# Splitting attention outputs at the accumulator, and one ring for raw weights and key tiles

## The chip, the cores and the metric

The kernel runs on one core of one Trainium2 chip. The metric is device time in microseconds. Of the kernel before there are three runs, and the median counts; one further execution was taken with a profile.

## The reference

Two layers (DEPTH = 2) over x of 2048 rows by 1024 columns, all in float32. Cut to what matters:

```python
for l in range(DEPTH):
    mod = silu(c) @ w_ada[l] + b_ada[l]
    shift, scale, gate = split(mod, 3)
    h = rms_norm(x, norm_g[l]) * (1 + scale) + shift
    gq, gk, gv, glr, gz, dq, dk, dv, dz = split_columns(h @ w_in[l])
    # group A: gated linear attention, 4 heads, chunks of 64 rows
    gq, gk, gv = split(silu(causal_depthwise_conv([gq, gk, gv], conv_w[l])))
    o_gla = gla_branch(gq, gk, gv, glr, gz, ...)     # scan over chunks, rms_norm, * silu(gz)
    # group B: differential softmax attention, 4 heads, two maps of 64 columns each
    q, k = rms_norm(dq) * 64 ** -0.5, rms_norm(dk)
    s = q @ k.T, masked to chunks up to the query's
    o = (softmax(s[map 0]) - lam * softmax(s[map 1])) @ dv
    o_diff = rms_norm(o) * (1 - lam_init) * silu(dz)
    x = x + gate * ([o_gla, o_diff] @ w_out[l])
```

## The kernel before

The 2048 rows are worked through in four blocks of 512 rows (u = 0 to 3) for each of two layers, eight blocks in all. Large products are made in three passes. Each float32 operand is split into a high part, rounded to fp32r, and a low part, the rest; TensorE adds high x high, high x low and low x high in one accumulator. The normalised input is kept so in hhi and hlo, the weights in a tile w, whose two halves are hi and lo.

**Weights.** In the first block of a layer (u = 0) `weights()` loads a raw tile of 128 by 512 from HBM, ScalarE (ACT) casts it into hi, GpSimd (POOL) subtracts to get lo, and the pair is stored to a buffer in HBM, called wd. The later blocks load the finished pair from wd. There are 72 such tiles in a layer: 8 for each of four attention heads (items 0 to 3), 8 for each of two groups of the gated branch (4 and 5), 8 for its gate (6), and 16 for the two halves of the output projection (7 and 8). Raw tiles have a ring of three (p_raw), finished ones a ring of four (p_w). One tile is one step of a projection: 12 matmuls of 128x512.

**A head of attention.** `head_evac` copies queries and keys out of the accumulators into rw, squares and sums them, takes the power -1/2 on POOL, and writes the normalised values into a new tile qk. `qk_gen` transposes these on TensorE, first the queries (g = 0), then the keys (g = 1), and splits them into qh and ql, and into a key tile Kt. `attn_gen` computes scores, softmax on DVE and ACT, and the product with the values. In later blocks it also loads the key tiles Kj of the earlier blocks. Kt and Kj share a ring of five (tag "K" of p_kv). At the end `to_oT` transposes the output of the head into an accumulator of the ring tp and ACT scales it into a tile oT.

**Output projection.** `out_gen` runs for block u after the input of the next block is prepared. It goes twice over eight oT tiles, once for each half of the output columns, and each time splits the tile again: ACT casts it into oh, DVE subtracts to get ol.

**Order.** The program is recorded by six streams (`run_streams`), which take turns by a clock of TensorE costs (`pe(0.65)` for a quarter of a step) and by events with a lag. For instance the transposes of a head wait in `qk_gen` for

```python
yield need("hev", key, hd, lag=6.0)
```

The recorded operations are then put in order for each engine by `Program.order`, a list scheduler with a cost model. Among the operations that are ready it takes the one recorded first. A tile of a ring gets a place only in the order in which the tiles were recorded, and only when an operation on it is ready otherwise:

```python
if b not in slot and (place[b] != nxt[t] or not slots[t]):
    blocked[t].append(i)
    break
```

Every engine, and the one DMA queue that SP issues, then works through its list strictly in that order. Most operations are recorded by `Program.issue`, so the profile gives nearly all of them line 284, and groups are told apart by the names of their tiles.

Of the kernel before, what the change touches and what calls it, by code (L numbers as in the profile page):

```python
# [11 lines left out]
F32 = mybir.dt.float32  # L12
F32R = mybir.dt.float32r
BF16 = mybir.dt.bfloat16
AF = mybir.ActivationFunctionType
ALU = mybir.AluOpType
# [4 lines left out]
P = 128  # L21
D = 1024
KT = D // P
UT = 512
# [4 lines left out]
C_GQ, C_GV, C_GLR, C_GZ, C_D = 0, 512, 1024, 1040, 1552  # L29
# [258 lines left out]
def trunk_kernel(ctx, tc, x, c, w_ada, b_ada, norm_g, w_in, conv_w, w_gk, b_gk, gla_norm_g,  # L288
# [10 lines left out]
    p_h = pool("p_h", 1)  # L299
    p_x = pool("p_x", 1)  # L300
    p_t = pool("p_t", 3)
    p_raw = pool("p_raw", 3)
    p_w = pool("p_w", 4)
    p_oT = pool("p_oT", 8)
    p_s = pool("p_s", 4)
    p_at = pool("p_at", 3)
    p_kv = pool("p_kv", 5)
    p_q = pool("p_q", 5)
# [209 lines left out]
    def run_streams(streams):  # L518
        st = [dict(g=g, ready=0.0, need=None) for g in streams]
        while st:  # L520
# [19 lines left out]
            else:  # L540
# [8 lines left out]
                assert nxt, [e["need"] for e in st]  # L549
                clock[0] = max(min(nxt), clock[0]) + 1e-6  # L550

    def weights(l, u, item, k, src, n=None):
        w = p_w.tile([P, 2, 512], F32R, tag="w", name="w")
        hi, lo = w[:, 0, :], w[:, 1, :]
        kept = WD[l][item][k]
        if u > 0:
            SY.dma_start(w.bitcast(F32), kept)
            return hi, lo
        raw = p_raw.tile([P, 512], F32, tag="raw", name="raw")
        SY.dma_start(raw if n is None else raw.rearrange("p (g n) -> p g n", n=n), src)  # L560
        A.copy(hi, raw)
        G.tensor_tensor(lo, raw, hi.bitcast(F32), op=ALU.subtract)
        if NU > 1:
            SY.dma_start(kept, w.bitcast(F32))
        return hi, lo
# [69 lines left out]
    def proj_T(l, u, item, col, banks):  # L635
        hhi, hlo = state["hhi"], state["hlo"]
        for k in range(KT):
            hi, lo = weights(l, u, item, k, w_in[l, k * P:(k + 1) * P, col:col + 512])
            for j in range(4):
                cs = slice(j * P, (j + 1) * P)  # L640
                if k == 0:
                    banks.append(acc())
                T.matmul(banks[j], hi[:, cs], hhi[k], start=(k == 0), stop=False)
                T.matmul(banks[j], hi[:, cs], hlo[k], start=False, stop=False)
                T.matmul(banks[j], lo[:, cs], hhi[k], start=False, stop=(k == KT - 1))
                yield pe(0.65)
# [17 lines left out]
    def to_oT(blocks, gain):  # L664
        ps = tp()
        for t in range(TT):
            T.transpose(ps[:, t * P:(t + 1) * P], blocks[t], ident)
        o2 = p_oT.tile([P, UT], F32, tag="oT", name="oT")
        A.activation(o2, ps, AF.Copy, scale=gain)
        return o2  # L670

    GL = {}

# [159 lines left out]
    oTs = {}  # L833
    HD = {}

    def head_evac(l, u, hd, banks):
        key = l * NU + u
        ss = p_sm.tile([P, TT, 4], F32, tag="qss", name="qss", bufs=2)
        rq = p_sm.tile([P, TT, 4], F32, tag="rq", name="rq", bufs=2)
        sz = p_z.tile([P, TT, P], F32, tag="z", name="z")  # L840
        Vt = p_kv.tile([P, TT, P], F32, tag="V", name="Vt")
        qk = []
        for t in range(TT):
            rw = p_t.tile([P, 256], F32, tag="rw", name="rw", bufs=4)
            A.copy(rw, banks[t][:, 0:256])
            th = p_t.tile([P, P], F32, tag="th", name="th", bufs=2)
            A.activation(th, banks[t][:, 384:512], AF.Tanh, scale=0.5)
            V.scalar_tensor_tensor(sz[:, t, :], th, 1.0, banks[t][:, 384:512], op0=ALU.add, op1=ALU.mult)
            A.copy(Vt[:, t, :], banks[t][:, 256:384])
            sq = p_t.tile([P, 256], F32, tag="sq", name="sq", bufs=2)  # L850
            A.activation(sq, rw, AF.Square)
            V.tensor_reduce(ss[:, t, :], sq.rearrange("p (a n) -> p a n", a=4), axis=AX.X, op=ALU.add)
            V.tensor_scalar(ss[:, t, :], ss[:, t, :], 1.0 / 64, EPS, op0=ALU.mult, op1=ALU.add)
            G.tensor_tensor(rq[:, t, :], ss[:, t, :], mhalf[:, 0:4], op=ALU.pow)
            n = p_q.tile([P, 256], F32, tag="qk", name="qk", bufs=4)
            V.tensor_tensor(n.rearrange("p (a n) -> p a n", a=4), rw.rearrange("p (a n) -> p a n", a=4),
                            rq[:, t, :].unsqueeze(2).to_broadcast([P, 4, 64]), op=ALU.mult)
            qk.append(n)
        HD[key, hd] = (qk, Vt, sz)

    def qk_gen(l, u, hd):
# [151 lines left out]
    def dense_gen(l, u, items):  # L1013
        key = l * NU + u
        yield need("h", key, lag=2.0)
        def gla_proj(grp):
            banks = []
            yield from proj_T(l, u, 4 + grp, C_GQ + 512 * grp, banks)
            if grp == 0:
                yield need("gate", key)  # L1020
            else:
                yield need("ktr", key)
            GL[f"cv{grp}"] = conv_evac(l, u, grp, banks)
            done("conv", key, grp)

        def head_proj(hd):
            def ld(k):
                src = w_in[l, k * P:(k + 1) * P, C_D:C_D + 2048].rearrange("p (g n) -> p g n", n=512)
                return weights(l, u, hd, k, src[:, :, hd * P:hd * P + P], n=P)

            banks = []
            yield from proj_N(ld, banks)
            if hd == LAST:
                done("free_h", key + 1)
            if hd >= 1:
                yield need("qkT", key, hd - 1)
            if hd >= 2:
                yield need("attn", key, hd - 2)
            head_evac(l, u, hd, banks)
            done("hev", key, hd)  # L1040

        def gate_proj():
            banks = []
            yield from proj_N(lambda k: weights(l, u, 6, k, w_in[l, k * P:(k + 1) * P, C_GZ:C_GZ + 512]), banks)
            if LAST == 4:
                done("free_h", key + 1)
            yield need("scan", key)
            osb = GL["osb"]
            for t in range(TT):
                sz = t2()  # L1050
                silu2(sz, banks[t])
                G.tensor_tensor(osb[:, t, :], osb[:, t, :], sz, op=ALU.mult)
            done("gz", key)

        LAST = 4
        for it in items:
            if it < 4:
                yield from head_proj(it)
            elif it < 6:
                yield from gla_proj(it - 4)  # L1060
            else:
                yield from gate_proj()

    def out_gen(l, u):
        y = layers[l]
        key = l * NU + u
        xsrc, xdst = io(l)
        final = key == L * NU - 1
        for hf in range(2):
            cs = slice(hf * 512, hf * 512 + 512)  # L1070
            banks = []
            for n_, k in enumerate((4, 5, 6, 0, 1, 2, 3, 7)):
                yield need("oT", key, 0 if k < 4 else k, lag=0.8)
                if n_ == 4:
                    rt = p_o.tile([P, TT, 512], F32, tag="osb", name="rt")
                    SY.dma_start(rt, xsrc(u)[:, cs].rearrange("(t p) n -> p t n", p=P))
                hi, lo = weights(l, u, 7 + hf, k, w_out[l, k * P:(k + 1) * P, cs])
                oh = p_oT.tile([P, UT], F32R, tag="oh", name="oh", bufs=2)
                ol = p_oT.tile([P, UT], F32R, tag="ol", name="ol", bufs=2)
                A.copy(oh, oTs[key, k])  # L1080
                V.tensor_tensor(ol, oTs[key, k], oh.bitcast(F32), op=ALU.subtract)
                for t in range(TT):
                    ts_ = slice(t * P, (t + 1) * P)
                    if n_ == 0:
                        banks.append(acc())
                    mm3(banks[t], oh[:, ts_], ol[:, ts_], hi, lo, n_ == 0, n_ == KT - 1)
                    yield pe(0.65)
            yield need("ada", l, 2)
            xo = xdst(u)[:, cs].rearrange("(t p) n -> p t n", p=P)
            for t in range(TT):  # L1090
                gy = t2()
                V.tensor_tensor(gy, banks[t], y.gate[:, cs], op=ALU.mult)
                if final and hf == 1:
                    V.tensor_tensor(rt[:, t, :], gy, rt[:, t, :], op=ALU.add)
                    SY.dma_start(xo[:, t, :], rt[:, t, :])
                    continue
                G.tensor_tensor(rt[:, t, :], gy, rt[:, t, :], op=ALU.add)
                if t % 2:
                    SY.dma_start(xo[:, t - 1:t + 1, :], rt[:, t - 1:t + 1, :])
        done("x", key)  # L1100
# [88 lines left out]
```

## Time and profile before

| | |
|---|---|
| median of 3 runs | 2660.28 us (2659.81 to 2660.94) |
| profiled execution | 2664.22 us |
| its span, first to last instruction | 2662.5 us |
| mean granted TensorE clock in it | 0.993 |
| TensorE (PE) busy | 2573.6 us, 97% |
| VectorE (DVE) busy | 1768.3 us, 66% |
| ScalarE (ACT) busy | 1207.0 us, 45% |
| GpSimd (POOL) busy | 625.3 us, 23% |
| DMA | 476.12 MB, mean 179 GB/s |

A row of a group reads: line, engine, operation, output <- inputs by the program's names, shapes, count, then busy time and mean length of one in ns, then the engine's idle time just before such instructions and what ended most of it. In the timeline a row begins with start and duration in us, and an idle time before it stands in brackets. The ends of matmuls are modelled, so consecutive ones overlap in the rows.

### The profile page before, as it was taken

The numbers are of one execution on the slowest core, as the hardware profiler recorded it, in microseconds if no ns is written. First come the engines' busy times: TensorE is split into PE (matmuls) and PEld (weight loads), VectorE is DVE, ScalarE is ACT, GpSimd is POOL, SyncE is SP. The second block draws the span as 40 slices with busy tenths as digits, with TensorE's granted clock in tenths as the row PEclk, the third lists the DMA queues.
The fourth block names the chain that finished last, engine by engine and source line by source line (L and its number), as shares of the span: only waits on it lengthen the run. The fifth ranks groups of instructions, "written<-read, shape, count | busy, mean of one in ns | idle before, by whom it ended". The sixth has DMA issues, their size and how long they took to land. (4 is left out here: it accounts for less than half of the span.)

```text
span 2662.5 us, 41105 instructions
## 1 busy us (share of the span) xinstructions
PE 2573.6 (97%) x13987; PEld 2070.3 (78%) x13987; DVE 1768.3 (66%) x5104; ACT 1207.0 (45%) x2592; POOL 625.3 (23%) x852
## 2 busy tenths in 40 slices
PE   7999899999999999999999989999999999999997
PEld 4777678877888778887777767887788877888886
DVE  4778757873767837676738764667637786387764
ACT  3555524453444533444634563344614456154442
POOL 2455411121010210102154554111121111210111
PEclk9999999999999999999999999999999999999998
DMA  8766586446552465334277656443374433734242
GB/s 278 243 229 240 205 295 198 160 154 213 170 186 96 151 206 171 139 131 136 83 263 250 230 202 244 163 175 139 124 262 151 150 130 112 265 121 153 91 139 103
DMA packets 201613, 476.12 MB, mean 179 GB/s; under 512 B 20735, under 2 KB 78269, under 8 KB 201405
## 3 DMA queue, kind: packets, MB, share of 16 engines
q1 hardware_dynamic: 201404, 473.50, 52.1%
q8 instruction: 111, 1.82, 0.3%
q14 instruction: 98, 0.79, 0.1%
HBM read 362.29 MB, written 111.15 MB: 178 GB/s over the span
## 5 line engine op out<-in xcount | busy, mean ns | idle before, releaser
L284 PE MATMUL acc<-w,hhi 128*128 128x512 f32 x2560 | 844.5, 405 | 5.9 <-DMA w<-wd 2.8
L284 PEld LDWEIGHTS acc<-w,hhi 128*128 128x128 f32 x2560 | 462.5, 189 | 106.0 <-issue 13.1
L284 PE MATMUL acc<-w,hlo 128*128 128x512 f32 x1280 | 507.4, 398 | 0.0
L284 ACT ACTIVATE s<-s,mx 128x512 f32<-128x512 f32 (+15 forms) x256 | 308.0, 1204 | 342.7 <-DVE s L284 341.3
L284 PE MATMUL acc<-hhi,w 128*128 128x512 f32 x1024 | 373.6, 406 | 1.2 <-DVE z L284 0.5
L284 PE MATMUL acc<-w,oh 128*128 128x512 f32 x1024 | 335.8, 403 | 8.6 <-DVE t L284 4.7
L284 DVE TENSOR_SCALAR_CACHE_REDUCE s<-sc,mx 64x64 f32<-64x64 f32 (+5 forms) x640 | 307.5, 485 | 43.6 <-PE sc L284 25.2
L284 PEld LDWEIGHTS acc<-w,hlo 128*128 128x128 f32 x1280 | 241.2, 188 | 51.1 <-issue 2.0
L284 POOL MEMSET s<- 64x64 f32 x256 | 39.0, 154 | 1027.3 <-DVE s L284 463.7
L284 POOL TENSOR_TENSOR w<-raw,w 128x512 fp32r<-128x512 f32 x144 | 195.0, 1364 | 194.1 <-ACT w L284 171.3
L284 PEld LDWEIGHTS acc<-w,oh 128*128 128x128 f32 x1024 | 191.2, 191 | 53.7 <-DVE t L284 8.5
L284 PEld LDWEIGHTS acc<-hhi,w 128*128 128x128 f32 x1024 | 192.5, 188 | 41.7 <-issue 1.2
L284 ACT COPY aT<-tp 128x512 f32<-128x512 f32 (+2 forms) x320 | 162.7, 520 | 115.5 <-PE tp L284 111.7
L284 PE MATMUL po<-Vj,aT 128*128 128x128 f32 x1536 | 205.2, 277 | 4.9 <-ACT aT L284 4.8
L284 PE MATMUL acc<-w,ol 128*128 128x512 f32 x512 | 202.9, 400 | 0.9 <-DVE ol L284 0.7
L284 PE MATMUL acc<-hlo,w 128*128 128x512 f32 x512 | 203.0, 396 | 0.0
L284 DVE TENSOR_SCALAR_CACHE_REDUCE s<-sc 128x512 f32<-128x512 f32 (+4 forms) x256 | 158.5, 623 | 66.9 <-PE sc L284 62.5
L284 PEld LDWEIGHTS po<-Vj,aT 128*128 128x128 f32 x1536 | 191.6, 193 | 14.6 <-ACT aT L284 9.1
L284 DVE SCALAR_TENSOR_TENSOR s<-s,r 128x512 f32<-128x512 f32 (+2 forms) x320 | 200.6, 676 | 2.9
L284 DVE TENSOR_TENSOR ol<-oT,oh 128x512 fp32r<-128x512 f32 x128 | 105.2, 828 | 120.2 <-ACT oh L284 108.7
L284 PE MATMUL tp<-ident,s 128*128 128x128 f32 x1088 | 172.5, 274 | 11.8 <-DVE s L284 9.4
L284 POOL TENSOR_TENSOR rq<-qss,mhalf 128x4 f32<-128x4 f32 x128 | 128.9, 1026 | 192.8 <-DVE qss L284 192.4
(167 smaller groups left out, 4209.2 us busy)
## 6 DMA issues: line engine op xcount, KB each, us to landing
w<-wd SPq DMA_DIRECT2D x432, 512.0 KB, 3.6
wd<-w SPq DMA_DIRECT2D x144, 512.0 KB, 3.4
raw<-in_w_in_dram SPq DMA_DIRECT2D x112, 256.0 KB, 4.3
Kj<-kd SPq DMA_DIRECT2D x48, 512.0 KB, 5.0
wr<-in_w_ada_dram SPq DMA_DIRECT2D x128, 128.0 KB, 3.2
kd<-Kt SPq DMA_DIRECT2D x24, 512.0 KB, 2.8
Vj<-vd SPq DMA_DIRECT2D x48, 256.0 KB, 4.1
xt<-in_x_dram SPq DMA_DIRECT2D x16, 512.0 KB, 3.8
```

The costliest lines, as they stand in the source:

```text
L284: getattr(self.engines[e], method)(*[real(a) for a in args], **{k: real(v) for k, v in kw.items()})
```

## The change

Three things are changed together.

- `to_oT` writes both parts of the split: ACT writes the scaled high part oh from the accumulator, and DVE computes scale x accumulator minus oh into ol. `out_gen` reads these pairs in both halves and no longer splits. The ring of eight oT tiles and two each of oh and ol becomes eight each of oh and ol.
- The ring p_raw goes. In u = 0 every even step takes one tile of the ring of key tiles, and loads two raw tiles into its halves, one for this step and one for the next.
- `head_evac` normalises queries and keys in rw itself; the ring of four qk tiles goes.

```diff
-    p_raw = pool("p_raw", 3)
     p_w = pool("p_w", 4)
-    p_oT = pool("p_oT", 8)
+    p_oT = pool("p_oT", KT)
...
+    raws = {}
+
     def weights(l, u, item, k, src, n=None):
...
-        raw = p_raw.tile([P, 512], F32, tag="raw", name="raw")
-        SY.dma_start(raw if n is None else raw.rearrange("p (g n) -> p g n", n=n), src)
+        if k % 2 == 0:
+            raws[k // 2] = p_kv.tile([P, 2, 512], F32, tag="K", name="raw")
+            for j in range(2):
+                raw = raws[k // 2][:, j, :]
+                SY.dma_start(raw if n is None else raw.rearrange("p (g n) -> p g n", n=n), src(k + j))
+        raw = raws[k // 2][:, k % 2, :]
         A.copy(hi, raw)
         G.tensor_tensor(lo, raw, hi.bitcast(F32), op=ALU.subtract)
...
-        o2 = p_oT.tile([P, UT], F32, tag="oT", name="oT")
-        A.activation(o2, ps, AF.Copy, scale=gain)
-        return o2
+        oh = p_oT.tile([P, UT], F32R, tag="oh", name="oh")
+        ol = p_oT.tile([P, UT], F32R, tag="ol", name="ol")
+        A.activation(oh, ps, AF.Copy, scale=gain)
+        V.scalar_tensor_tensor(ol, ps, gain, oh.bitcast(F32), op0=ALU.mult, op1=ALU.subtract)
+        return oh, ol
...
-            n = p_q.tile([P, 256], F32, tag="qk", name="qk", bufs=4)
-            V.tensor_tensor(n.rearrange("p (a n) -> p a n", a=4), rw.rearrange("p (a n) -> p a n", a=4),
-                            rq[:, t, :].unsqueeze(2).to_broadcast([P, 4, 64]), op=ALU.mult)
-            qk.append(n)
+            rv = rw.rearrange("p (a n) -> p a n", a=4)
+            V.tensor_tensor(rv, rv, rq[:, t, :].unsqueeze(2).to_broadcast([P, 4, 64]), op=ALU.mult)
+            qk.append(rw)
...
-                oh = p_oT.tile([P, UT], F32R, tag="oh", name="oh", bufs=2)
-                ol = p_oT.tile([P, UT], F32R, tag="ol", name="ol", bufs=2)
-                A.copy(oh, oTs[key, k])
-                V.tensor_tensor(ol, oTs[key, k], oh.bitcast(F32), op=ALU.subtract)
+                oh, ol = oTs[key, k]
```

The callers of `weights` now pass a function of the step instead of one source; the DMAs are the same ones.

More of the change, by code (lines that the diff above doesn't have):

```diff
@@ L637, in proj_T @@
         for k in range(KT):
-            hi, lo = weights(l, u, item, k, w_in[l, k * P:(k + 1) * P, col:col + 512])
+            hi, lo = weights(l, u, item, k, lambda k: w_in[l, k * P:(k + 1) * P, col:col + 512])
             for j in range(4):
@@ L1026, in head_proj, with src @@
         def head_proj(hd):
+            def src(k):
+                cols = w_in[l, k * P:(k + 1) * P, C_D:C_D + 2048].rearrange("p (g n) -> p g n", n=512)
+                return cols[:, :, hd * P:hd * P + P]
             def ld(k):
-                src = w_in[l, k * P:(k + 1) * P, C_D:C_D + 2048].rearrange("p (g n) -> p g n", n=512)
-                return weights(l, u, hd, k, src[:, :, hd * P:hd * P + P], n=P)
+                return weights(l, u, hd, k, src, n=P)
             banks = []
@@ L1043, in gate_proj @@
             banks = []
-            yield from proj_N(lambda k: weights(l, u, 6, k, w_in[l, k * P:(k + 1) * P, C_GZ:C_GZ + 512]), banks)
+            src = lambda k: w_in[l, k * P:(k + 1) * P, C_GZ:C_GZ + 512]
+            yield from proj_N(lambda k: weights(l, u, 6, k, src), banks)
             if LAST == 4:
@@ L1076, in out_gen @@
                     SY.dma_start(rt, xsrc(u)[:, cs].rearrange("(t p) n -> p t n", p=P))
-                hi, lo = weights(l, u, 7 + hf, k, w_out[l, k * P:(k + 1) * P, cs])
-                oh = p_oT.tile([P, UT], F32R, tag="oh", name="oh", bufs=2)
-                ol = p_oT.tile([P, UT], F32R, tag="ol", name="ol", bufs=2)
-                A.copy(oh, oTs[key, k])
-                V.tensor_tensor(ol, oTs[key, k], oh.bitcast(F32), op=ALU.subtract)
+                hi, lo = weights(l, u, 7 + hf, k, lambda k: w_out[l, k * P:(k + 1) * P, cs])
+                oh, ol = oTs[key, k]
                 for t in range(TT):
```

## The prediction

> **What bounds the kernel now.** I read the page first, then the stages by windows, then the groups, then single stretches of the timeline.
>
> ```profile
> span 2662.5 us, 41105 instructions
> PE 2573.6 (97%) x13987; PEld 2070.3 (78%) x13987; DVE 1768.3 (66%) x5104; ACT 1207.0 (45%) x2592; POOL 625.3 (23%) x852
> ```
>
> TensorE is busy 97% of the span, so what the change takes from DVE and ACT is worth only the time for which TensorE waits for them. The change alters none of TensorE's own matmuls: it can win at most what TensorE idles, and lose by making it idle more. Where it idles is shown by windows (columns: stretch, its length, then PE, PEld, DVE, ACT and POOL busy, granted clock, DMA share, GB/s):
>
> ```profile
> 24.00:72.00 48.00, 43.31 (x249) 30.06 (x241) 24.04 (x70) 19.00 (x36) 13.09 (x13) 0.96 0.82 273
> 276.00:343.00 67.00, 61.99 (x275) 45.81 (x276) 47.75 (x80) 34.65 (x60) 30.17 (x23) 0.95 0.65 220
> 1584.00:1648.00 64.00, 59.65 (x274) 45.96 (x274) 35.31 (x64) 35.01 (x61) 30.08 (x25) 0.97 0.59 207
> 1990.00:2320.00 330.00, 329.44 (x1840) 270.29 (x1839) 217.90 (x649) 150.92 (x313) 54.46 (x88) 1.00 0.47 160
> ```
>
> A whole later block of 512 rows (1990 to 2320 us) idles 0.6 us: nothing can be won there. The first block of each layer (u = 0, where raw weights are loaded and split) is loose: the output projections of those blocks, the second and third rows, idle 5.0 and 4.4 us and lose clock besides (67 x 0.05 = 3.4 us, 64 x 0.03 = 1.9 us). Only these stretches, the start and the two ends of attention can move.
>
> **The split of the attention outputs.** Its groups now:
>
> ```profile
> L284 PE MATMUL acc<-w,oh 128*128 128x512 f32 x1024 | 335.8, 403 | 8.6 <-DVE t L284 4.7 <-ACT oh L284 4.0
> L284 PE MATMUL acc<-w,ol 128*128 128x512 f32 x512 | 202.9, 400 | 0.9 <-DVE ol L284 0.7
> L284 ACT CAST oh<-oT 128x512 fp32r<-128x512 f32 x128 | 79.0, 623 | 147.6 <-PE acc L284 146.9
> L284 DVE TENSOR_TENSOR ol<-oT,oh 128x512 fp32r<-128x512 f32 x128 | 105.2, 828 | 120.2 <-ACT oh L284 108.7 <-PE acc L284 11.1
> L284 DVE SCALAR_TENSOR_TENSOR ql<-tp,G,qh 64x512 fp32r<-64x512 f32 x64 | 48.0, 749 | 59.4 <-ACT qh L284 58.2 <-PE sc L284 0.3
> ```
>
> Removed: 128 casts on ACT (79.0 us) and 128 subtractions on DVE (105.2 us). Added: 64 DVE operations that scale an accumulator and subtract; the nearest row is ql, the same operation from PSUM over as many columns, 749 ns, so 64 x 0.75 = 48 us. The 64 ACT copies that left the accumulators stay, only writing another type. DVE loses 57 us and ACT 79 us, nearly all beside TensorE's work. On the path stand the waits: 4.0 us for oh and 0.7 us for ol; the 4.7 us for DVE t are accumulators not yet emptied, and stay. Nearly all of the 4.0 us is two stalls, one at the end of each layer's attention. The second, by the timeline:
>
> ```profile
> 2627.26 0.69 ACT L284 ACTIVATE oT<-tp,dg 128x512 f32<-128x512 f32 x1 [1.62 <-PE tp L284]
> 2627.85 1.12 ACT L284 CAST oh<-oT 128x512 fp32r<-128x512 f32 x2
> 2629.03 1.22 PE L284 MATMUL acc<-w,oh 128*128 128x512 f32 x2 [1.80 <-ACT oh L284]
> ```
>
> With oh written by the first instruction, the matmul starts after 2627.95 instead of 2628.97 us: 1.0 us each, 2.1 for both. With the remaining 0.4 + 0.7 us that is 3.2 us. The two u = 0 output projections lose 16 x 0.62 = 9.9 us of ACT work each; I take a third of their 9.4 us of idle, 3.1 us. Together **-6.3 us**, between -3 and -14 (the waits, with all that idle and half the lost clock).
>
> Some of DVE's removed time is blocking, which these rows show:
>
> ```profile
> 292.37 1.76 DVE L284 TENSOR_TENSOR ol<-oT,oh 128x512 fp32r<-128x512 f32 x1
> 290.61 4.65 POOL L284 TENSOR_TENSOR w<-raw,w 128x512 fp32r<-128x512 f32 x3
> L284 DVE TENSOR_TENSOR ol<-oT,oh x128: 676/692/1807, 121.1 to 2651.5; 128x512 fp32r<-128x512 f32 x128
> ```
>
> A subtraction beside POOL's took 1.76 us against a median of 0.69. The Trainium skill says (SBUF — State Buffer, section Who interferes with whom) that a DVE instruction with two SBUF inputs waits for a whole GpSimd instruction that reads SBUF, and one with a single SBUF input does not. By it the new operation, with one input in PSUM, would never take 1.8 us, and the gain in these two stretches would lie nearer its far end. The trace agrees in the 1.76 us row.
>
> **Normalising in place.** Same DVE operation, same size, no copy. A rw tile is now held until its transposes; these run within the first steps of the next projection (at 143.25 us below), and the next head is evacuated only after all 96 matmuls of its own. Cost nothing; if that cover went, the wait would be ACT's copy of the next head's accumulators. The larger oT ring is written out one block later than it is read: nothing.
>
> **The ring of key tiles.** Before, three raw tiles had a ring of their own. Now a pair of them takes one of five places that the key tiles Kt and Kj also take, strictly in the order in which the program records them, and order() gives a tile its place only when its first instruction is ready. For Kt that is after the second group of the head's transposes (tp<-ident,qk). So the raw pair recorded behind a Kt can't be requested before those transposes. By the lags in the code (6.0 after the evacuation, 2.6 per weight step), Kt is recorded two to four steps into the next projection, so TensorE has that much to do before it needs the blocked pair. Eight Kt stand so: four heads in u = 0 of two layers. From the blocked request to full use the pair needs
>
> ```profile
> raw<-in_w_in_dram SPq DMA_DIRECT2D x112, 256.0 KB, 4.3
> L284 ACT CAST w<-raw 128x512 fp32r<-128x512 f32 x144 | 88.8, 625 | 90.7 <-PE acc L284 38.2 <-DMA raw<-in_w_in_dram 28.8 <-DMA raw<-in_w_out_dram 7.0
> L284 POOL TENSOR_TENSOR w<-raw,w 128x512 fp32r<-128x512 f32 x144 | 195.0, 1364 | 194.1 <-ACT w L284 171.3 <-issue 13.1 <-DMA w<-wd 9.6
> ```
>
> 4.3 + 0.6 + 1.4 = 6.3 us. Against it stands the time from the transposes to the matmul that uses that step in the run of before. The five Kt where it is shorter (each: the transposes, then the row in which the blocked step begins; in the first, third and fourth its first matmul is the second of the two):
>
> ```profile
> 143.25 0.60 PE L284 MATMUL tp<-ident,qk 128*128 128x128 f32 x4
> 145.56 0.63 PE L284 MATMUL acc<-hhi,w 128*128 128x512 f32 x2
> ...
> 203.22 0.60 PE L284 MATMUL tp<-ident,qk 128*128 128x128 f32 x4
> 204.34 0.73 PE L284 MATMUL acc<-w,hhi 128*128 128x512 f32 x2
> ...
> 1395.49 0.60 PE L284 MATMUL tp<-ident,qk 128*128 128x128 f32 x4
> 1397.79 0.63 PE L284 MATMUL acc<-hhi,w 128*128 128x512 f32 x2
> ...
> 1456.56 0.60 PE L284 MATMUL tp<-ident,qk 128*128 128x128 f32 x4
> 1458.87 0.63 PE L284 MATMUL acc<-hhi,w 128*128 128x512 f32 x2
> ...
> 1557.19 0.60 PE L284 MATMUL tp<-ident,qk 128*128 128x128 f32 x4
> 1562.58 0.62 PE L284 MATMUL acc<-w,hhi 128*128 128x512 f32 x2
> ```
>
> The step would come late by 6.3 - 2.5 = 3.8, 6.3 - 1.1 = 5.2, 3.8, 3.8 and 0.9 us: 17.5 us. TensorE can fill it with the first four score pairs of that head:
>
> ```profile
> 146.83 0.33 PE L284 MATMUL sc<-Kt,qh 128*128 128x128 f32 x1 [0.65 <-DVE Kt L284]
> 147.11 0.45 PE L284 MATMUL acc<-hlo,w 128*128 128x512 f32 x1
> ```
>
> A pair lasts 0.28 us until the next matmul, so four fill 1.1 us: 17.5 - 4 x 1.1 - 0.9 = 12.2 us idle. Such idle also lowers the clock: in the stretch 276 to 343 us, with 5.0 us of idle, 3.4 us of clock went. I count half of that, 1.7 us, for every second of the four stalls: 3.4 us. Sum **+15.6 us**; between 0 (attention and the gated branch fill all) and 17.5 + 4 x 1.7 = 24 us. SP's queue, past which the raws move, holds the stores wd behind them; they have as much slack as before.
>
> The Trainium skill says (TensorE: Matmul & The Clock Gate, Part 1) that the clock halves after an idle window of about 3.4 us. The 0.95 above agrees that idle costs clock. By that rule, with stalls of 2.7 to 4.1 us, four windows of half clock would be an estimate of the most that can follow.
>
> **The start.** Ten raw tiles instead of three can be requested before the second half of the first modulation weights:
>
> ```profile
> 16.88 2.51 SPq L284 DMA_DIRECT2D raw<-in_w_in_dram  x3
> 22.32 8.54 SPq L284 DMA_DIRECT2D wr<-in_w_ada_dram  x6
> ```
>
> Seven more at 2.51 / 3 = 0.84 us delay that second half by 5.9 us; the weight steps that wait for raws later get them early, which can take back the 4.7 us of idle between 24 and 72 us. I take 0, between -4.7 and +5.9 us.
>
> **Sum.** -6.3 + 15.6 + 0 = +9.3 us. The profiled execution took 2664.2 us, 1.7 around its span, 3.9 us above the median of the runs; on its scale 2673.5 us, on the median's 2660.3 + 9.3 = 2669.6, say 2669 us.
>
> **Rivals.** Faster: the ring costs nothing, because after the transposes other work is ready for TensorE for 4 us or more (the head's scores, the scan of the gated branch at 203 us, whose po<-Sn matmuls run between), and the deeper prefetch takes back the start's 4.7 us. Place: the five steps above; it decides when the blocked step follows the transposes by 6.3 us without an idle row before it. Then -6.3 - 4.7 = 2649 us. Against it: at 145.6 and 1397.8 us nothing but the projection runs.
>
> Same: half the lateness is filled, 6 us, against -6.3: 2660 us.
>
> Much slower: all 24 us of the ring and 5.9 us of the start, less 6.3: 2684 us. For it: the start's DMA share of 0.82; against it, late raws come in bursts that catch up.
>
> The split isn't free: an accumulator of the ring tp is now held by ACT and then DVE, 0.75 us longer, 64 times. If every third is wanted at that moment: 16 us, with the ring's 6 filled to half and the split's -6.3, 2676 us. For it, PE's waits for tp exist; against it, the ring has four banks.
>
> **How the numbers follow.** Forecast 0.37 (2664 to 2676), faster 0.34, same 0.13, much slower 0.12, bank held 0.04. A measurement of this kernel can tell about 0.2%, 5.3 us. Faster by more: 0.34. Within: the same case and the forecast's low edge, 0.16. Slower: 0.50. The range takes in the rival at 2649 with its gain at -14 cut off, and the much slower case at 2684 with little more: 2644 to 2688 us.
>
> **What would show it.** In the profile after: no oh<-oT; 64 ol<-tp of about 0.75 us; PE's idle before acc<-w,oh near 5 us; the stalls at the ends of attention about 1 us shorter; the first block's dense matmuls (acc<-hhi,w, acc<-w,hhi) waiting for ACT w, POOL w or DMA raw just after the heads' qk transposes, near 3 us each; ten raws issued in a row at the start. If those waits are missing, the ring's term is wrong and the time falls below 2660.

## The result and the profile after

| | after | before |
|---|---|---|
| median | 2666.61 us (20 runs, 2658.44 to 2671.43) | 2663.39 us (20 runs, 2657.64 to 2668.79) |
| ratio after / before | 1.0012, 95% interval 1.0005 to 1.0019 | |
| profiled execution, span | 2662.56 us, 2660.8 us | 2664.22 us, 2662.5 us |

The change costs 3.2 us. That lies below the 5.3 us which the prediction called the least that one can tell; with 20 runs of each the interval leaves out 1 all the same. The sign holds for these runs only: one program's ratio differed by 0.2% between runs on two chips (below, in the experiment on the start), and that is more than this 0.12%. Runs of one kernel lie up to 13 us apart, and the profiled run of after is on its quick side. So the two spans below don't show the loss; they are read for where time moved, and the medians for how much.

The page of after, its span and its busy times:

```profile
span 2660.8 us, 40667 instructions
PE 2571.6 (97%) x13987; PEld 2077.1 (78%) x13987; DVE 1710.9 (64%) x5040; ACT 1134.4 (43%) x2464; POOL 622.0 (23%) x852
```

DVE lost 57.4 us and ACT 72.6 us (57 and 79 were forecast), and TensorE's idle stayed what it was: 88.9 us before, 89.2 after. The groups of after that answer to those of the prediction:

```profile
L284 PE MATMUL acc<-w,hhi 128*128 128x512 f32 x2560 | 845.2, 406 | 3.8 <-ACT ub L284 1.9 <-DVE t L284 0.9 <-ACT w L284 0.8
L284 PE MATMUL acc<-hhi,w 128*128 128x512 f32 x1024 | 374.5, 408 | 0.4 <-DVE z L284 0.2
L284 PE MATMUL acc<-w,oh 128*128 128x512 f32 x1024 | 332.2, 400 | 4.4 <-DVE t L284 2.8 <-ACT oh L284 1.6
L284 PE MATMUL acc<-w,ol 128*128 128x512 f32 x512 | 203.5, 398 | 0.1
L284 DVE SCALAR_TENSOR_TENSOR ol<-tp,dg,oh 128x512 fp32r<-128x512 f32 x32 | 23.9, 747 | 6.6 <-ACT oh L284 6.3
L284 DVE SCALAR_TENSOR_TENSOR ol<-tp,gg,oh 128x512 fp32r<-128x512 f32 x32 | 23.7, 744 | 0.3 <-ACT oh L284 0.2
```

The waits for oh fell from 4.0 to 1.6 us and those for ol from 0.7 to nothing; with the other waits, the idle time before the two rows went from 8.6 to 4.4 and from 0.9 to 0.1 us. But the first two rows hold nothing of what the ring was to cost: the dense matmuls wait 0.8 us for ACT w, and not at all for POOL w or a raw tile. The ring's price must be elsewhere. Windows over the first block of layer 0, first of before and then of after (stretch, length, PE, PEld, DVE, ACT and POOL busy, granted clock, DMA share, GB/s):

```profile
24.00:355.00 331.00, 302.86 (x1554) 227.42 (x1547) 233.46 (x612) 160.83 (x378) 153.50 (x164) 0.98 0.72 244
```

```profile
24.00:355.00 331.00, 300.07 (x1523) 230.75 (x1516) 220.37 (x603) 152.28 (x362) 149.70 (x162) 0.95 0.68 235
286.00:353.00 67.00, 62.62 (x283) 47.09 (x284) 39.26 (x80) 27.96 (x47) 28.76 (x23) 0.95 0.59 211
1587.00:1651.00 64.00, 60.96 (x301) 47.58 (x302) 27.81 (x61) 30.73 (x56) 31.55 (x28) 1.00 0.62 222
```

In the same 331 us after gets 31 fewer matmuls done and idles 2.8 us more (30.9 for 28.1), and its clock is 0.95 instead of 0.98: 331 x 0.03 = 9.9 us. At the end of this block after is 9.3 us behind: the next block's first matmul starts at 354.65 us, in before at 345.39. That is less than the 12.7 us of idle and clock together, since half clock costs nothing while TensorE stands (0.88 of the clock with PE at 0.00, in the row at 151.36 us below). It makes that good later: the output projections of the first blocks idle 4.4 and 3.0 us (5.0 and 4.4 before), and in layer 1's the clock is 1.00 instead of 0.97. So in this execution the loss lies in layer 0's first block alone, and later stages give it back. One execution says this only roughly: three kernels below (Kt early, in layer 0 alone, and with held places) have the same lists up to 1318 us but for a few small writes, and start the next block at 349.20, 344.37 and 345.86 us.

Why TensorE waits in that block is in the timeline. First SP's queue, before and then after:

```profile
139.18 0.32 SPq L284 DMA_DIRECT2D wd<-w  x1
139.59 0.38 SPq L284 DMA_DIRECT2D raw<-in_w_in_dram  x1
140.61 0.32 SPq L284 DMA_DIRECT2D wd<-w  x1
141.02 0.43 SPq L284 DMA_DIRECT2D raw<-in_w_in_dram  x1
```

```profile
124.78 13.96 SPq L284 DMA_DIRECT2D wd<-w  x4
140.51 0.32 SPq L284 DMA_DIRECT2D vd<-Vt  x1
144.37 0.32 SPq L284 DMA_DIRECT2D wd<-w  x1
144.74 4.40 SPq L284 DMA_DIRECT2D raw<-in_w_in_dram  x8
```

Before, a store and a raw take turns. After, no raw is requested from 106.5 to 144.7 us, 38 us long, since the planned list has them behind the stores; then eight come at once. Then all engines of after in the same stretch:

```profile
148.43 0.60 PE L284 MATMUL tp<-ident,rw 128*128 128x128 f32 x4
148.94 1.35 POOL L284 TENSOR_TENSOR w<-raw,w 128x512 fp32r<-128x512 f32 x1 [4.59 <-ACT w L284]
149.06 1.51 DVE L284 CAST ql<-ql 64x512 fp32r<-64x512 f32 x1
...
150.97 0.40 PE L284 MATMUL acc<-hhi,w 128*128 128x512 f32 x1
151.07 4.08 POOL L284 TENSOR_TENSOR w<-raw,w 128x512 fp32r<-128x512 f32 x3 [0.79 <-DMA raw<-in_w_in_dram]
151.37 1.25 DVE L284 CAST qh<-qh 64x512 fp32r<-64x512 f32 x1
152.55 1.48 DVE L284 CAST ql<-ql 64x512 fp32r<-64x512 f32 x1
154.06 1.41 DVE L284 TENSOR_TENSOR Kt<-tp,Kt 64x512 fp32r<-64x512 f32 x2
154.80 0.48 PE L284 MATMUL sc<-Kt,qh 128*128 128x128 f32 x1 [3.44 <-DVE Kt L284]
```

The burst makes POOL subtract in a row just when DVE copies the halves of qh and ql. DVE works through its list in order, so Kt, behind the copies, comes late, and TensorE stands for 3.44 us with a ready weight beside it: the next dense matmul is behind the scores in its list. The same copy in before began 0.11 us ahead of the subtraction beside it, and was not held up:

```profile
143.88 0.41 DVE L284 CAST ql<-ql 64x512 fp32r<-64x512 f32 x1
143.99 1.45 POOL L284 TENSOR_TENSOR w<-raw,w 128x512 fp32r<-128x512 f32 x1 [2.17 <-ACT w L284]
```

Before isn't free of it: of its 16 such copies in this block two were held up, 0.63 and 1.51 us long, against five in after, 0.63 to 1.51 us.

The Trainium skill says (SBUF — State Buffer, section Who interferes with whom) that copies and casts of DVE can enter a mode that uses the port pair shared with GpSimd, and that whoever comes second is held for the whole instruction of the other. The trace agrees: the cast at 149.06 came second and ended 0.28 us after POOL's subtraction, 1.51 us in place of 0.41; at 143.88 us in before the cast came first, and the subtraction took 1.45 us in place of 1.3.

The stall also costs clock. Windows of after, around this stall and around a shorter one:

```profile
151.36:154.80 3.44, 0.00 (x2) 0.00 (x1) 3.36 (x4) 0.62 (x2) 3.44 (x3) 0.88 1.06 313
154.80:161.00 6.20, 6.20 (x19) 5.28 (x20) 3.85 (x21) 1.59 (x6) 0.50 (x2) 0.51 0.76 237
161.00:168.00 7.00, 7.00 (x36) 5.78 (x35) 3.27 (x17) 4.05 (x12) 3.39 (x6) 1.00 0.89 316
```

```profile
208.00:215.00 7.00, 4.54 (x37) 3.06 (x32) 5.67 (x14) 3.14 (x5) 0.98 (x2) 1.00 0.73 198
215.00:219.00 4.00, 3.71 (x12) 3.08 (x12) 3.78 (x15) 2.81 (x8) 2.13 (x3) 0.57 1.13 346
```

A stall of 3.44 us was followed by 6.2 us at half clock, 3.0 us of work lost. Before 215 us TensorE had idled only 2.46 of 7 us, then 0.29 us more, and half clock came too.

### The profile page after: what moved, and what is told of

It is laid out like the page before. It is cut to its first block, busy times and chain, and to the rows that moved or that the text cites. A ratio compares the mean times of both kernels' runs of the same rounds, so it can differ in the third digit from the quotient of the medians.

```text
span 2660.8 us, 40667 instructions
## 1 busy us (share of the span) xinstructions
PE 2571.6 (97%) x13987; PEld 2077.1 (78%) x13987; DVE 1710.9 (64%) x5040; ACT 1134.4 (43%) x2464; POOL 622.0 (23%) x852
## 4 chain that ended last, share of the span: by engine, by line
PE 79%; DVE 13%; DMA 2%; issue 2%; ACT 2%; POOL 1%; SPq 0%; DVEq 0%; ACTq 0%; POOLq 0%
PE acc L284 50%; PE sc L284 12%; PE po L284 10%; PE tp L284 7%; DVE s L284 4%; DVE t L284 3%; DMA wr<-in_w_ada_dram 2%; DVE ql L284 1%; DVE am L284 1%; DVE hlo L284 1%; DVE hhi L284 1%; DVE r L284 1%; ACT s L284 0%; POOL rq L284 0%; DVE z L284 0%
## 5 line engine op out<-in xcount | busy, mean ns | idle before, releaser
L284 PEld LDWEIGHTS acc<-w,hhi 128*128 128x128 f32 x2560 | 464.0, 189 | 101.1 <-issue 12.2
L284 ACT COPY rw<-acc 128x256 f32<-128x256 f32 x128 | 50.1, 391 | 289.6 <-PE acc L284 288.3
```

Of the source, the lines that this page charges most:

```text
L284: getattr(self.engines[e], method)(*[real(a) for a in args], **{k: real(v) for k, v in kw.items()})
```

## The experiments

Theory R (theory A in the expectations): the ring costs time because blocked raws come late, by the order in which Kt and the pairs take their places. What the first trace left open is how a late raw costs: through the dense matmuls that use it (the prediction's form), through POOL's burst beside DVE's copies (theory C), or through half clock that any idle of some us brings on, with the copies no more than one cause (theory D). Further rivals: the split or the in-place step costs by itself; the requests at the start cost. All ratios are to before, with medians of before from the same chip and session.

**In place alone**, on the kernel before.

```diff
-            n = p_q.tile([P, 256], F32, tag="qk", name="qk", bufs=4)
+            rv = rw.rearrange("p (a n) -> p a n", a=4)
...
-            qk.append(n)
+            qk.append(rw)
```

> The kernel before with one part of the change, normalising in rw itself. All theories: no change, 2663 us within 2 us of the kernel before (ratio 0.9992 to 1.0008), dense stages of the first block within 1 us of before.

Measured 2663.44 us, before 2664.49; 0.999 (0.9981 to 0.9999). Free, as forecast.

**The ring and in place, without the split**: `to_oT` and `out_gen` as before.

```diff
-        oh = p_oT.tile([P, UT], F32R, tag="oh", name="oh")
-        ol = p_oT.tile([P, UT], F32R, tag="ol", name="ol")
...
+        o2 = p_oT.tile([P, UT], F32, tag="oT", name="oT")
+        A.activation(o2, ps, AF.Copy, scale=gain)
```

> The whole change but the split: outputs are split twice in the output projection as before; raw pairs share the ring of key tiles. Theory A (a raw pair recorded behind a Kt waits for that Kt's place, and costs TensorE time in the first block of layer 0; the split gives about 6 us back): 2672 us, ratio 1.003 to 1.0045, the changed kernel 5 to 8 us faster than this one; the output projection of layer 0's first block still starts 10 to 13 us late. Rival B (the ring costs nothing, the slower start or the split's longer hold of accumulators is what costs): within 2 us of the kernel before, if the split costs; or equal to the changed kernel at 2666 us, if the start does.

Measured 2675.13 us, before 2664.49; 1.0034 (1.002 to 1.0049). Against in place alone the ring costs 11.7 us, and the split (1.0012 after, from another session) gives back 0.22%, 5.9 us. In its trace 8.8 us of the ring's loss stand at the end of layer 0's first block already, of 11.9 us between the spans; the other 3.1 us came later.

**Pairs requested two pairs earlier.** In the output projection of the first blocks, whose steps go out of order, this kernel multiplies other raw tiles than the right ones.

```diff
-        if k % 2 == 0:
-            raws[k // 2] = p_kv.tile([P, 2, 512], F32, tag="K", name="raw")
+        for i in range(0 if k == 0 else k // 2 + 2, min(KT // 2, k // 2 + 3)) if k % 2 == 0 else ():
+            raws[i] = p_kv.tile([P, 2, 512], F32, tag="K", name="raw")
```

> The changed kernel, but each raw pair is requested two pairs (four steps) earlier in the record, so that the pairs that stood behind a Kt now stand ahead of it. Theory A: the stalls before Kt's scores near 92 and 151 us and the half-rate clock between 72 and 220 us go, the output projection of layer 0's first block starts 8 to 13 us earlier than in the changed kernel, and the time falls by 7 to 12 us to 2654 to 2660 us, below the kernel before. Rival B (start or split): no change, 2666 us. Rival C (the loss is a burst of eight raws whose subtractions on POOL hold up DVE, whatever the place): bursts are smaller but not gone, 2663 us.

Measured 2659.67 us, before 2664.49; 0.9981 (0.997 to 0.9992).

**Kt takes its place before the transposes**, in `head_evac` of the first blocks, by writing one element.

```diff
+        Kt = None
+        if u == 0:
+            Kt = p_kv.tile([P, 2, UT], F32R, tag="K", name="Kt")
+            V.memset(Kt[0:1, 0, 0:1].bitcast(F32), 0.0)
...
-        Kt = p_kv.tile([P, 2, UT], F32R, tag="K", name="Kt")
+        if Kt is None:
+            Kt = p_kv.tile([P, 2, UT], F32R, tag="K", name="Kt")
```

> The changed kernel, but in the first block of a layer Kt takes its place in the ring at the head's evacuation (by a write of one element), so no raw pair waits for it; requests are not made any earlier in the record. Theory A: as with requests four steps earlier, 2654 to 2660 us, and no raw is requested within 2 us of a head's second transposes as now. Rival B: 2666 us. Rival C (bursts): between.

Measured 2658.52 us, before 2664.49; 0.9974 (0.9963 to 0.9985). Two different edits that end the block turn the loss into a gain, so theory R holds as far as that goes: late requests cost. A sign that was expected did not come, though: raws still go out near a head's second transposes (two from 143.47 us, transposes at 144.48). They go by twos now, where after has eight in a row; with pairs requested earlier five still go in a row at 146.75 us.

**The same in layer 0 alone, and in layer 1 alone** (`if u == 0 and l == 0`, then `l == 1`).

> As e4_kt_early, but Kt takes its early place only in the first block of layer 0. From the changed kernel's trace (its first block of layer 0 falls 9.8 us behind the kernel before, that of layer 1 gains 4.6 us): nearly the whole gain of e4_kt_early lies here, ratio to the kernel before 0.997 to 0.9985. If instead both layers pay alike, as the prediction's working had it (two stalls of 3.8 and one of 0.9 us in layer 1): half the gain, ratio 0.999 to 1.000.

> As e4_kt_early, but only in the first block of layer 1. If the block costs in layer 0 alone: as the changed kernel, ratio 1.000 to 1.002. If both pay alike: 0.999 to 1.000.

Measured 2655.19 us, 0.9963 (0.995 to 0.9975), and 2664.87 us, 1.0001 (0.9992 to 1.001); before 2664.06. Layer 0 holds the gain. In layer 1 the early Kt is worth nothing that can be told: its trace waits longer for Kt there, 4.5 us where after waits 1.9. So three of the five late pairs, those of layer 1, cost nothing that can be told.

**Raws in a ring of their own, of two single tiles**, with split and in place; two small constants move to other rings.

```diff
+    p_raw = pool("p_raw", 2)
...
+        raw = p_raw.tile([P, 512], F32, tag="raw", name="raw")
+        SY.dma_start(raw if n is None else raw.rearrange("p (g n) -> p g n", n=n), src(k))
```

> The split and the normalising in place, with raw tiles in a ring of their own again, of two single tiles instead of three (two constants of the start live in rings that are free then). Key tiles have their ring to themselves. Theory A: the split's 6 us without the ring's cost, less what a ring of two loses in prefetching: 2657 to 2662 us, ratio 0.997 to 0.9995. If deep prefetch is what makes e4_kt_early fast: 2664 us or more.

Measured 2687.89 us, before 2664.06; 1.0085 (1.0071 to 1.0099): missed by 26 us. I had taken two tiles to be deep enough. The waits of TensorE in this kernel (total us, times, longest):

```profile
PE acc L284 <- ACT w L284: 7.4, 6, 3.6
PE tp L284 <- DVE xt L284: 7.2, 1, 7.2
PE acc L284 <- POOL w L284: 5.0, 12, 1.2
```

Here the waits that the prediction gave the shared ring do appear, 12.4 us of them. The expectation gave 2664 us or more as the sign that deep prefetch is what makes the early Kt fast. It came, but it doesn't decide that: two tiles are fewer than the three of before, and some of the loss may be the moved constants', so neither the depth nor the sharing is priced here.

**Kt early and the input projections' pairs two pairs ahead.**

> Both cures together: Kt placed at the evacuation, and raw pairs of the input projection requested four steps earlier. If a single cause was at work (the blocked request), no further gain over e4_kt_early, ratio 0.9965 to 0.9985; if earlier requests help for a reason of their own, 0.996 or less.

Measured 2658.93 us, before 2664.06; 0.9981 (0.997 to 0.9991). The two cures don't add.

**The four copies per head on ACT**, on after, in layer 0's first block. They no longer stand in DVE's list ahead of Kt, nor beside POOL's subtractions.

```diff
-                    V.tensor_copy(qh[other, m, :], qh[own, m, :].bitcast(F32))
-                    V.tensor_copy(ql[other, m, :], ql[own, m, :].bitcast(F32))
+                    if l == 0 and u == 0:
+                        A.copy(qh[other, m, :], qh[own, m, :].bitcast(F32))
+                        A.copy(ql[other, m, :], ql[own, m, :].bitcast(F32))
```

> The changed kernel, with the four copies of qh and ql in the first block of layer 0 on ACT instead of DVE. Theory C (the late raws' subtractions on POOL hold up these DVE copies, and with them the scores and TensorE): 2660 to 2663 us, ratio 0.999 to 1.000. Theory D (the cost is time at half clock, brought on by any idle of some us near the heads' starts; DVE's copies are 2.8 us longer in all and no more than one cause of it): as the changed kernel, 1.0005 to 1.002, and some 30 us at half clock in that block as now.

Measured 2658.78 us, before 2664.6; 0.9984 (0.9975 to 0.9993), 0.28% below after and more than either theory forecast. Raws are as late as in after: eight from 141.51 us, 3.7 us before the second transposes. But more than the copies has moved: ACT's casts of raws now stand behind them, and POOL's row of three subtractions begins only at 149.23 us, with the scores.

**The start: Kt early in layer 0, and three places of the ring kept until the third part of the start.**

```diff
+        held = [p_kv.tile([P, 2, UT], F32, tag="K", name="held") for _ in range(3)]
+        for h_ in held:
+            V.memset(h_[0:1, 0, 0:1], 0.0)
...
+            if c == 2:
+                for h_ in held:
+                    V.memset(h_[0:1, 0, 0:1], 0.0)
```

> As e5_kt_early_l0, but three of the ring's five places are held until the third part of the first modulation is done, so that four raw tiles instead of ten are requested at the start. If the ten early requests help (in e5_kt_early_l0 the ninth weight step starts at 59 us, in the kernel before at 73): 5 to 10 us slower than e5_kt_early_l0, ratio 0.998 to 1.000. If they only delay the modulation weights (the prediction's fear): as e5_kt_early_l0 or faster, 0.9945 to 0.997.

Measured 2661.08 us, before 2664.6; 0.9983 (0.9974 to 0.9991). This tested nothing: nothing ties the second writes to the step they follow, so all six were done at once, and as many raws were requested early as in the kernel that it was to differ from. First this kernel, then that one:

```profile
16.95 8.04 SPq L284 DMA_DIRECT2D raw<-in_w_in_dram  x8
```

```profile
16.97 8.06 SPq L284 DMA_DIRECT2D raw<-in_w_in_dram  x8
```

All else stands in the same order on every engine, but for two small writes of DVE near 2.4 us that change places. So it is a repetition of the Kt-early-in-layer-0 kernel on another chip, and differs from it by 0.2% (0.9983 and 0.9963). Ratios of different sessions are therefore good to about 0.2% here, wider than their intervals; the ring's 0.44% is above that and was taken in one session, the split's 0.22% is not.

**Both: Kt early in layer 0 and the copies on ACT.**

> e5_kt_early_l0 and the copies on ACT together. Theory C: another 1 to 3 us, 0.995 to 0.996. Theory D: as e5_kt_early_l0, 0.9955 to 0.997.

Measured 2648.46 us (2644.93 to 2656.41, 6 runs), before 2664.6; 0.9944 (0.9931 to 0.9957). It beats both kernels. In one session the copies are worth 0.39% (0.9983 to 0.9944); the 0.28% on after, from two sessions, can't be told from it.

**The control: the copies on ACT, on the kernel before.**

> The kernel before, with nothing but the four copies of qh and ql per head on ACT instead of DVE in the first block of layer 0. Theory: the copies hurt after because the ring lets raw weights come in bursts, so that POOL's subtractions run in rows beside DVE's copies, in the chain that ends in the key tile. In the kernel before raws come evenly, so there is little to win: 0.999 to 1.000 of before, 2661 to 2665 us, and in the first block of layer 0 no milestone earlier by more than 2 us. Rival: the copies hurt in any kernel with 16 splits of raw weights per two heads on POOL, whatever the ring: 0.997 of before or less, 2657 us or less, as the same edit took 0.28% off after. Second rival: ACT, which makes the high parts of the weights there, becomes late by the copies: above 1.001.

Measured 2663.13 us, before 2665.31; 0.9991 (0.9982 to 1.0). Little or nothing, where raws come evenly from a ring of their own. One part of the expectation failed: the output projection of the first block starts at 274.02 us, 2.4 earlier than in before, and the next block 4.0 earlier, in one trace of each. The same row in 24 to 355 us, TensorE's first scores of a head and their wait for Kt, in before, after, without the split, copies on ACT (on after), both, and the control:

```profile
L284 PE MATMUL sc<-Kt,qh 128*128 128x128 f32 x8 | 2.3, 290 | 2.0 <-DVE Kt L284 2.0
```

```profile
L284 PE MATMUL sc<-Kt,qh 128*128 128x128 f32 x8 | 2.8, 345 | 5.9 <-DVE Kt L284 5.9
```

```profile
L284 PE MATMUL sc<-Kt,qh 128*128 128x128 f32 x8 | 2.8, 350 | 5.8 <-DVE Kt L284 5.8
```

```profile
L284 PE MATMUL sc<-Kt,qh 128*128 128x128 f32 x8 | 2.2, 271 | 4.1 <-DVE Kt L284 4.1
```

```profile
L284 PE MATMUL sc<-Kt,qh 128*128 128x128 f32 x8 | 2.5, 312 | 3.1 <-DVE Kt L284 3.1
```

```profile
L284 PE MATMUL sc<-Kt,qh 128*128 128x128 f32 x8 | 2.3, 290 | 1.4 <-DVE Kt L284 1.4
```

In these six rows the wait is longer with the ring, whether or not the split is there, and shrinks with the copies' move. The medians speak for theory C and against D, which forecast no gain from that move; the waits of dense matmuls have no part in it. But the wait for Kt doesn't carry the loss. The same row with Kt early in layer 0:

```profile
L284 PE MATMUL sc<-Kt,qh 128*128 128x128 f32 x8 | 2.6, 321 | 4.6 <-DVE Kt L284 4.6
```

That kernel beats before, and yet it waits nearly as long as after; three of its copies took 1.51 to 1.52 us. The opposite case is Kt early in layer 1 alone, which has after's lists up to 1326 us. It waited 1.8 us for Kt in this row, no longer than before, and its next block still began at 351.29 us, 5.9 us behind:

```profile
24.00:355.00 331.00, 303.71 (x1541) 232.27 (x1534) 221.56 (x607) 152.67 (x363) 151.31 (x164) 0.96 0.69 238
```

It idles no more than before (27.3 and 28.1 us); what it loses is clock. So half clock is the larger part of the cost in these traces, as theory D had it: over this stretch the clock is 0.95 to 0.96 in the three traces of the ring with late requests, 0.97 to 0.98 where Kt or the requests come early, 0.97 with only the copies moved, and 0.98 to 0.99 in before, in place alone and the control. In the move of the copies, too, the row's wait falls by 1.8 us from after, while the medians fall by 7.8 us. The same block of the kernel with both edits:

```profile
24.00:355.00 331.00, 307.06 (x1597) 234.62 (x1590) 216.74 (x595) 162.64 (x378) 151.17 (x164) 0.99 0.73 250
```

0.99 against 0.95 is 13 us in these 331. Which idle times bring half clock on with the ring, and how much of that is POOL beside DVE's copies, the runs don't settle; the profiled run of this kernel is its slowest.

## Why the prediction was right in sign and wrong in size

The total moved the forecast way, by a third of the forecast, and less than one program's ratio differs between two chips; so its sign isn't strong support.

- **The split, -6.3 us: right as far as can be told.** Medians give -5.9 us, known to about 5. Its far end of -14 is a slip: the waits, all that idle and half the lost clock (3.2 + 9.4 + 2.7) make -15.3. The instruction counts and 0.75 us of the new operation came out; none of the 64 took over 0.752 us. The bank-held rival's waits show, but are small: TensorE waited four times for ol before it could write tp, 1.2 us in all, where 16 were put. The stalls at the ends of attention fell by 1.0 us each, as worked out; the second:

```profile
2627.36 0.69 ACT L284 ACTIVATE oh<-tp,dg 128x512 fp32r<-128x512 f32 x1 [1.63 <-PE tp L284]
2628.10 0.77 PE L284 MATMUL acc<-w,oh 128*128 128x512 f32 x2 [0.78 <-ACT oh L284]
```

- **In place, 0: right**, 0.999.
- **The ring, +15.6 us: right in sign, too large, and wrong in form.** The failed step is "the raw pair recorded behind a Kt can't be requested before those transposes". That is the planner's rule, not SP's: in its list the burst at 144.74 us went out 3.7 us before the second transposes at 148.43, because on the chip a request waits only for what used the place before. So the weights were ready in time (the first of the burst's at 150.29 us, its step began at 150.97) and the five latenesses, 17.5 us, did not happen. What remained of the plan is the order of the lists: raws behind stores, then eight at once. In after's trace POOL then ran beside DVE's copies ahead of Kt; how much of the 11.7 us goes that way stays open.
- **Where:** I spread the ring's idle over both layers. Most of it came in layer 0; layer 1's three pairs, put at 8.5 us, cost nothing that the medians can tell.
- **Idle against clock:** I had 12.2 us of idle and 3.4 of clock. After's trace, with the split in it, has 2.8 us more idle in layer 0's first block and 9.9 us of clock: 12.7 us. The term's 11.7 us by the medians is thus nearer to 15.6 than its parts are to theirs, and that is luck: the sum was made of latenesses that did not happen.
- **The signature failed as a test.** I wrote that without the dense waits the time falls below 2660. They are missing, and the time didn't fall: I had not asked what else late raws collide with.
- **The start, 0:** ten raws were issued in a row, as said:

```profile
16.73 9.54 SPq L284 DMA_DIRECT2D raw<-in_w_in_dram  x10
```

Its value was never measured by itself.
- **The faster rival** is what the kernel becomes when the block is removed: Kt early in layer 0 gives 3.5 to 8.9 us less than before in three kernels, short of the 11 us worked out.

## What to carry to other kernels

When buffers share one ring, the order in which a planner hands out places becomes the order of the DMA queue; look in the queue's timeline for gaps followed by bursts, and then for what the burst's consumers run beside. Weights that arrive just in time can still cost. Here a port, the order of a list and the clock had a part, and the clock the largest. Giving the late-written tile (Kt) its place early, and moving DVE copies out of the burst's way to ACT, turned +0.12% into -0.56%.

## What the runs showed of the hardware

- Casts on DVE of 64x512 took 0.41 to 0.42 us alone or when they began first, and 0.63 to 1.51 us when a subtraction of POOL was under way as they began; the operation with one input in PSUM stayed at 0.75 us, also in the seven of 64 that ran beside such a subtraction.
- Half clock came after less than 3 us of idle. Before 215 us it was 2.46 us within 7 us and 0.29 more, and 0.57 of the clock followed. In the stall from 151.36 to 154.80 us the clock was 1.00 from 153 to 154 us and 0.50 from 154 to 155, so it halved after 2.6 us. The Trainium skill (TensorE: Matmul & The Clock Gate, Part 1) puts it after an idle window of about 3.4 us. Neither case agrees, unless idle is summed over a window in a way that the rows can't show.
- One list of instructions, but for six writes of one element and two small writes that changed places, ran 0.2% apart on two chips, each against its own before.
